# Weight sums at each stage's beginning, u one stage ahead, exponentials behind z's silu, and seven products for the first pool pair

## The chip, the cores and the metric

The kernel runs on one core of one Trainium2 chip. The metric is the device time in microseconds of one execution, the median of three runs. The engines of the core are named as in the profile: PE is TensorE (its matmuls; PEld are its weight loads), DVE is VectorE, ACT is ScalarE, POOL is GpSimd and SP is SyncE. Each engine works through its own queue in order; a DMA is issued from the queue of one of the engines, here SP, POOL or ACT.

## The reference, cut to what matters

512 tokens and 16 meta tokens ahead of them go through one layer of a hybrid decoder: a projection of all features, a pooling branch, a state-space branch (Mamba-2, "SSD") in 8 groups, gates that merge the two, and an MLP.

```
u = rmsnorm(h, mix_norm_w)
proj = u @ w_in                       # pool | z | x,B,C | dt | gates
u_pool, z, xbc, dt_raw, gates = ...
y_pool = pool_mixer(u_pool, pool_w_group, pool_scale) @ w_pool_up
# mamba2_branch
xbc = silu(causal_depthwise_conv(xbc, conv_w, conv_b))
xs, b_mat, c_mat = ...
y = ssd_chunked(xs, dt, a, b_mat, c_mat) + xs * d_skip
y = y * silu(z)
y = y * rsqrt(mean over the group(y * y) + EPS) * norm_w
y_ssd = y @ w_ssd_out
h = h + (gate_pool * y_pool + gate_ssd * y_ssd) @ w_o
v = rmsnorm(h, mlp_norm_w)
h = h + square(relu(v @ w_ff1)) @ w_ff2
out = rmsnorm(h, final_norm_w)
```

The pooling branch has four groups of 256 features with windows of 2, 4, 8 and 16 positions; each takes the windowed mean of its own projection less the projection itself, and then a 256 x 256 matrix.

## The kernel before

*Products.* Every float32 operand is split into a rounded part and the remainder (hi and lo), and a product is three matmuls: hi with hi, hi with lo and lo with hi. A weight block of 1024 columns is loaded by SP into a tile `raw` (three buffers), cast to `whi` by ACT (L95), and subtracted to `wlo` by DVE (L97); both have four buffers. Features lie on the 128 partitions, tokens (528, or 512 without the meta tokens) along the free dimension, in two halves of 264 columns where all 528 are wanted. L197 and L199 are the matmuls of `proj`.

*Seven products.* Two weight blocks against two halves of u can be multiplied with seven products of 264 columns instead of eight. It needs sums of the weight blocks (T1, T2, S3, T4) and sums of u (`T["0", ...]`, `T["1", ...]`). The function `pair` does this for the x tiles of groups 4 to 7 (`X_PAIRS`): all seven products write one psum tile `pqx` of two banks, and after each, ACT or DVE takes the bank's value into `rax` or `rbx`. The sums of the weights are formed in DRAM, by DMAs on POOL's queue that copy a block and then accumulate another onto it (`weight_steps`; tiles `f_t`, `f_s`, `fx_t`, `fx_s`); the sums for the two MLP matrices, used at the end of the kernel, are made in the same way. The sums of u are formed by `sums_of_u`: two raw tiles of u come in by DMA on POOL's queue (`rau`, `rbu` from `u_d`), DVE combines them in four operations (L876 to L879), and ACT and DVE split the results. The function `pool_pair` does seven products for two tiles of a pool group, with the weights' sums formed by DVE; before, the first pool group treated, group 3, has its two tiles by `pool_tile` instead, each with its own weight block against both halves of u, 48 matmuls of 264 columns.

*Stages.* Stage g runs the state-space part of group g, `ssd(g)`, together with `group_proj(g + 1)`, which projects B, C (`px`), the two x tiles (`px`, or `pqx` as a pair), a gate tile in some groups (`pgp`), and z (`pz`, two halves in one psum tile, then ACT's silu into `zt`). The function `weave` takes one step of each generator in turn; engines then run in the order of the program, unless `issue_after` puts an instruction behind a named one of its engine. `ssd(g)` begins with transposes (`ptb`, `ptm`, `ptx`), loads a broadcast of the cumulated decay (`abc`, 1 MB, on POOL's queue), takes exponentials of it (`eb`, L609; masks in `abc`, L614, L620, L621), computes the states (`pst`, copied to `st` at L643), the two parts of y (`po`, `py`), multiplies by z's silu into `yt`, squares it (`sqg`, split to `qhg`, L311, and `qlg`), sums the squares on PE (`png`, L685 and L686), takes the reciprocal root (`rs`, L688), and splits the normed y into `yh` (L697) and `yl`. ACT's functions are exp, silu and the reciprocal root, and a change between them is an ACT_TABLE_LOAD.

*Around the stages.* In stage 4 `out_half` is woven in: the product with the first half of `w_ssd_out`, eight tiles of 512 columns in `pso`, copied to `so` (L806) and put into DRAM. In stage 7 `out_part` (`psp`) fills the place of the projection. Then come the pool stage (four groups in the order 3, 2, 1, 0), the rest of the gates, the merge, `w_o`, and the MLP.

*Where the weight sums' DMAs stand.* `weight_sums_at(SETS_AT[g], PIECES.get(g, 12))` spreads the DMAs of one or two sets over a stage's steps. Each is ordered behind a copy of one column of the latest result (`seen`, on POOL), so that it is not issued before the stage has come that far. `SETS_AT` gives the sets of the eight stages: 1, 1, 2, 1, 2, 2, 1, 1. psum has two buffers for tiles of two banks (`psum2`) and four for tiles of one (`psum1`).

*Where the exponentials stand.* `eb` of group g comes behind the silu of that group's x tiles (`x_ready`), and for groups 5 to 7 behind that of z (`z_ready`):

```
with tc.issue_after((z_ready if g in X_PAIRS[1:] else x_ready)[g].ins):
    act.activation(eb[js, :, :], ap[js, :, j, :], AF.Exp)
```

Of the kernel before, what the change touches and what calls it, by code (L numbers as in the profile page):

```python
# [14 lines left out]
P = 128  # L15
# [31 lines left out]

SUMS_AT = {0: (0,), 1: (1,), 2: (2, 3)}

# [3 lines left out]

SETS_AT = {0: 1, 1: 1, 2: 2, 3: 1, 4: 2, 5: 2, 6: 1, 7: 1}
PIECES = {4: 21, 7: 14}
SETS_POOL = 0

# [7 lines left out]
def kernel(ctx: ExitStack, tc, xT, x, w, fx, f1, f2, vec, fnw, out):  # L65
# [110 lines left out]
    def psum2(name):  # L176
        return psa.tile([P, 1024], F32, tag="mm", name=name)
# [32 lines left out]
    def narrow(ps):  # L210
        return [(ps, slice(NM, L))]
# [200 lines left out]
    mark = [None]  # L412
    x_ready, z_ready, filled = {}, {}, {}

    def conv(dst, src, ct):
        n = dst.shape[-1]
        e = src.shape[-1] - n
        act.activation(dst, src[:, e:], AF.Identity, bias=col(V_CB, ct), scale=col(V_CW, ct * 4 + 3))
        for j in range(1, 4):
            o = max(0, j - e)  # L420
            dve.scalar_tensor_tensor(dst[:, o:], src[:, e + o - j : e + n - j],
                                     col(V_CW, ct * 4 + 3 - j), dst[:, o:], op0=ALU.mult, op1=ALU.add)
        silu = act.activation(dst, dst, AF.Silu)
        mark[0] = dst[:, :1]
        if ct < 16:
            x_ready[ct // 2] = silu

# [44 lines left out]
    def pair(kind, g, r):  # L472
# [5 lines left out]
        for m, f, n, start, stop in MULTIPLY:  # L478
# [3 lines left out]
            for low in range(2):  # L482
                for k in range(4):
                    wk = wt[low][:, k * P : (k + 1) * P]
                    pe.matmul(o, wk, f[k][0], start=start and not low and k == 0,  # L485
                              stop=stop and low == 1 and k == 3, skip_group_check=True)
                    if not low:
                        pe.matmul(o, wk, f[k][1], start=False, stop=False, skip_group_check=True)
# [19 lines left out]
    def group_proj(g, cur, gate=None):  # L508
# [60 lines left out]
    def ssd(g, cur):  # L569
# [36 lines left out]
        for j in range(2):  # L606
            js = slice(64 * j, 64 * j + 64)
            with tc.issue_after((z_ready if g in X_PAIRS[1:] else x_ready)[g].ins):
                act.activation(eb[js, :, :], ap[js, :, j, :], AF.Exp)  # L609
# [94 lines left out]
    def weave(a, b, n, sums, side):  # L704

        end = object()
        a, sums = [a], [sums]
        while a or b or side:
            for t in [a] + [b] * n:
                for q in (t, sums):  # L710
                    if q and next(q[0], end) is end:
                        q.pop(0)
            side = [q for q in side if next(q, end) is not end]
        for q in sums:
            for _ in q:
                pass
# [25 lines left out]
    def weight_steps():  # L742
        t = sets.pop(0)
        src = {"fx": fx, "f1": f1, "f2": f2}[t[0]][t[1]]
        o = {n: wsum[(*t, n)] for n in SUMS[t[0]]}
        put = nc.gpsimd.dma_start
        yield put(o["t1"], src[B11])
        yield put(o["s3"], src[B12])
        yield put(o["t1"], src[B12], accum_op=ALU.add)
        if "t2" in o:  # L750
            yield put(o["t2"], src[B22])
        yield put(o["s3"], src[B22], accum_op=ALU.add)
        if "t2" in o:
            yield put(o["t2"], o["t1"], accum_op=ALU.add)
            yield put(o["t4"], src[B21])
            yield put(o["t4"], o["t2"], accum_op=ALU.add)

# [4 lines left out]

    def weight_sums_at(n, pieces):
        total = sum(2 * len(SUMS[t[0]]) for t in sets[:n])
        steps = (e for _ in range(n) for e in weight_steps())
        put = i = 0
        while put < total:
            i += 1
            if put * pieces < i * total:
# [3 lines left out]
                put += 1  # L773
            yield
        assert next(steps, None) is None

# [23 lines left out]
    def out_half():  # L800
        for dd in range(4):
            ps = psum2(f"pso{dd}")
            for i in range(2):
                ssd_out(2 * dd + i, ps[:, i * SEQ : (i + 1) * SEQ], range(8))
                o = staged(f"so{2 * dd + i}")
                act.copy(o, ps[:, i * SEQ : (i + 1) * SEQ])  # L806
                nc.scalar.dma_start(acc_d[2 * dd + i], o)
                mark[0] = o[:, :1]
                yield
# [51 lines left out]


    def sums_of_u(ks, g):

        one, two = HF

        def load(k):
            a, b = raw_pair("u", k)
            with tc.issue_after(abc_load[g].ins):
                for t, kk in ((a, k), (b, k + 4)):  # L870
                    nc.gpsimd.dma_start(t, u_d[kk])
            return a, b

        def combine(a, b, behind):
            with tc.issue_after(behind[g].ins):
# [4 lines left out]

        def form(k, n, src, behind):
            hi, lo = T[n, "h", k], T[n, "l", k]
# [40 lines left out]
    yps, last, copied, mixed = {}, {}, {}, []  # L923

    def pool_tile(t):
        win = WIN[t // 2]
        ps = psum2(f"pp{t}")

        skip = min(NM - win, NM - 4)
        runs, view = wide(ps, skip)  # L930
        proj(runs, block(), U)
        u = gp.tile([P, L + 8], F32, tag="pu", name=f"pu{t}", bufs=4)[:, :L]
        act.copy(u[:, skip:], view)
        return averaged(t, u)

# [92 lines left out]
    for d in range(NK):  # L1028
        t_load = nc.gpsimd.dma_start(acc[d], acc_d[d])
    for _ in range(SETS_POOL):  # L1030
        with tc.issue_after(t_load.ins):
            t_load = weight_sums()
    pend = [pooled_halves(*pool_tile(2 * POOL_ORDER[0] + i)) for i in range(2)]

# [783 lines left out]
```

## Time and profile before

| | us |
|---|---|
| median of three runs | 1017.71 |
| lowest and highest | 1017.05, 1018.7 |
| profiled execution | 1019.7 |
| its span | 1018.0 |
| PE busy | 998.0 |
| PE weight loads busy | 876.6 |
| DVE busy | 799.0 |
| ACT busy | 603.6 |
| POOL busy | 120.4 |

The span is the time from the first to the last instruction of the profiled execution. Busy times of different engines overlap. Matmuls are pipelined, so one is drawn longer than the distance to the next one's start. A row of the time line gives the start, the duration, the engine, the line of the kernel, the operation and its tiles, how many like it follow one another (x), and in brackets how long the engine stood idle before it and what ended that. A row of the table of stretches gives each engine's busy time and its number of instructions, the clock that TensorE was granted (1.00 is full speed), the busy share of the 16 DMA engines, and GB/s.

### The profile page before, as it was taken

What the parts mean: (1) busy time and instruction counts of PE and PEld (TensorE: products, weight loads), DVE (VectorE), ACT (ScalarE), POOL (GpSimd) and SP (SyncE); (2) the same over time, 40 slices, a digit from 0 to 9 for tenths busy, and PEclk for the clock granted to TensorE, in tenths of its full rate; (3) what the DMA queues carried; (4) which work ended last, traced back from release to release, by engine and by line L of the source; (5) the groups of instructions that cost most, each with busy time, mean ns of one, the idle gap of its engine ahead of it and who ended that gap; (6) DMA issues with size and microseconds to landing.
All of it is one profiled execution on the core that took longest, in us unless ns stands there. A gap on an engine that the chain in (4) does not pass through costs nothing.

```text
span 1018.0 us, 15702 instructions
## 1 busy us (share of the span) xinstructions
PE 998.0 (98%) x6047; PEld 876.6 (86%) x6047; DVE 799.0 (78%) x1153; ACT 603.6 (59%) x853; POOL 120.4 (12%) x215
## 2 busy tenths in 40 slices
PE   9999999999999999999999999999999999999997
PEld 7889888979788897987889888888889999999986
DVE  7968797778653787877689756877988888888885
ACT  8656769484833575665345533458656656665654
POOL 0001211212122212123400000221000000000000
PEclk9999999999999999999999999999999999999999
DMA  7265868566688748487933542879454554455432
GB/s 254 87 225 163 246 192 229 167 188 198 179 255 266 215 140 238 118 233 208 253 129 103 212 161 63 268 193 338 112 185 134 158 182 149 156 175 150 141 104 83
DMA packets 61803, 184.52 MB, mean 181 GB/s; under 512 B 7072, under 2 KB 8416, under 8 KB 60704
## 3 DMA queue, kind: packets, MB, share of 16 engines
q1 hardware_dynamic: 39456, 109.00, 32.3%
q0 software_dynamic: 18240, 67.51, 26.2%
q10 hardware_dynamic: 4032, 7.00, 1.9%
q8 instruction: 47, 0.77, 0.3%
q14 instruction: 28, 0.23, 0.1%
HBM read 173.13 MB, written 58.59 MB: 228 GB/s over the span
## 4 chain that ended last, share of the span: by engine, by line
PE 87%; ACT 6%; DMA 3%; DVE 2%; issue 1%; POOL 0%; ACTq 0%; DVEq 0%; POOLq 0%; SPq 0%
PE px L1437 8%; PE px L197 7%; PE alpha L1505 6%; PE px L1440 4%; PE px L199 4%; PE pz L197 4%; PE alpha L1508 3%; PE pgs L197 3%; PE pgp L197 2%; DMA raw<-in_w 2%; PE pqx L485 2%; PE py L667 2%; PE pz L199 2%; PE wo_alpha L1199 1%; PE pf L130 1%; PE pf L129 1%
## 5 line engine op out<-in xcount | busy, mean ns | idle before, releaser
L95 ACT CAST whi<-raw 128x1024 fp32r<-128x1024 f32 (+2 forms) x90 | 90.1, 1011 | 83.4 <-DMA raw<-in_w 18.1
L97 DVE TENSOR_TENSOR wlo<-raw,whi 128x1024 fp32r<-128x1024 f32 (+2 forms) x90 | 104.9, 1172 | 37.9 <-ACT whi L95 28.9
L197 PE MATMUL px<-uh,whi 128*128 128x264 f32 (+1 forms) x320 | 82.4, 295 | 0.0
L199 PE MATMUL px<-ul,whi 128*128 128x264 f32 (+1 forms) x320 | 79.9, 287 | 0.0
L1212 DVE TENSOR_TENSOR ht<-ht,alpha 128x1024 f32<-128x1024 f32 x35 | 42.7, 1219 | 29.1 <-PE alpha L1505 29.1
L197 PEld LDWEIGHTS px<-uh,whi 128*128 128x128 f32 x320 | 61.5, 192 | 1.3 <-issue 0.9
L199 PEld LDWEIGHTS px<-ul,whi 128*128 128x128 f32 x320 | 61.3, 192 | 0.3
L1135 ACT CAST shi<-rawf 128x1024 fp32r<-128x1024 f32 x42 | 44.2, 1053 | 28.7 <-PE alpha L1508 18.3
L1505 PE MATMUL alpha<-shi,hh 128*128 128x512 f32 x140 | 55.2, 394 | 0.0
L1508 PE MATMUL alpha<-shi,hl 128*128 128x512 f32 x140 | 54.7, 391 | 0.0
L1136 DVE TENSOR_TENSOR slo<-rawf,shi 128x1024 fp32r<-128x1024 f32 x42 | 51.2, 1218 | 0.6 <-ACT shi L1135 0.6
L1440 PE MATMUL px<-vsl,shi 128*128 128x256 f32 x192 | 47.4, 280 | 0.0
L1437 PE MATMUL px<-vsh,shi 128*128 128x256 f32 x192 | 47.4, 281 | 0.0
L197 PE MATMUL pz<-uh,whi 128*128 128x512 f32 x112 | 45.1, 402 | 1.5 <-ACT yh L697 1.3
L199 PE MATMUL pz<-ul,whi 128*128 128x512 f32 x112 | 44.6, 398 | 0.0
L197 PE MATMUL px<-uh,wlo 128*128 128x264 f32 (+1 forms) x320 | 42.5, 284 | 0.0
L197 PEld LDWEIGHTS px<-uh,wlo 128*128 128x128 f32 x320 | 40.1, 189 | 0.0
L1505 PE MATMUL alpha<-slo,hh 128*128 128x512 f32 x140 | 37.4, 389 | 0.0
L1437 PEld LDWEIGHTS px<-vsh,shi 128*128 128x128 f32 x192 | 36.2, 188 | 0.9
L1440 PEld LDWEIGHTS px<-vsl,shi 128*128 128x128 f32 x192 | 36.1, 188 | 0.9
L1440 PE MATMUL px<-vl,shi 128*128 128x256 f32 x144 | 36.1, 283 | 0.0
L1437 PE MATMUL px<-vh,shi 128*128 128x256 f32 x144 | 36.0, 282 | 0.0
(600 smaller groups left out, 3066.5 us busy)
## 6 DMA issues: line engine op xcount, KB each, us to landing
raw<-in_w SPq DMA_DIRECT2D x96, 512.0 KB, 4.9
f_t<-in_f POOLq DMA_DIRECT2D x38, 512.0 KB, 6.8
f_s<-in_f POOLq DMA_DIRECT2D x26, 512.0 KB, 7.4
b<-in_f SPq DMA_DIRECT2D x21, 512.0 KB, 4.6
rawf<-in_f SPq DMA_DIRECT2D x36, 256.0 KB, 3.0
rawf<-f_t SPq DMA_DIRECT2D x36, 256.0 KB, 2.9
abc<-acs_d POOLq DMA_DIRECT2D x8, 1024.0 KB, 7.6
f_t<-f_t POOLq DMA_DIRECT2D x12, 512.0 KB, 5.9
```

Source lines behind the costliest of these rows:

```text
L95: act.copy(hi[:, c], raw[:, c])
L97: dve.tensor_tensor(lo[:, c], raw[:, c], hi[:, c].bitcast(F32), op=ALU.subtract)
L197: pe.matmul(o, wt, rhs[0][k][:, c], start=part == 0 and k == 0, stop=part == 1 and k == NK - 1)
L199: mm[0] = pe.matmul(o, wt, rhs[1][k][:, c], start=False, stop=False)
L485: pe.matmul(o, wk, f[k][0], start=start and not low and k == 0, stop=stop and low == 1 and k == 3, skip_group_check=True)
L1135: splits.append((act.copy(hi, src), dve.tensor_tensor(lo, src, hi.bitcast(F32), op=ALU.subtract)))
L1136: dve.tensor_tensor(lo, src, hi.bitcast(F32), op=ALU.subtract)))
L1212: added[0] = dve.tensor_tensor(o, o, src, op=op)
L1437: pe.matmul(ps, m, f[k][0], start=start and not low and k == 0, stop=stop and low == 1 and k == 3, skip_group_check=True)
L1440: pe.matmul(ps, m, f[k][1], start=False, stop=False, skip_group_check=True)
L1505: pe.matmul(ps[t], hh[:, p, seg, st], m, start=bool(first and not low and p == 0), stop=bool(last and low and p == 1), skip_group_check=True)
L1508: pe.matmul(ps[t], hl[:, p, seg, st], m, start=False, stop=False, skip_group_check=True)
```

## The change

- *Weight sums.* One generator, `line`, runs over all sets. `paced(slots)` issues a given number of its DMAs at given steps of a stage: five at step 0, two at step 2, one at step 4; stage 4 has eight more at steps 9, 12 and 14, and stage 7 only two and two. Each slot has one `seen` copy on POOL. Within a set, or within two sets of the second MLP matrix, all copies are issued ahead of the accumulations. The number of sets that go through is the same.
- *Sums of u.* `sums_of_u` runs in stages 0, 1 and 2 as before, but with two of the four in stage 0, and the load of the next raw tiles is issued at the end of a sum, so that it is there when the next stage wants it. In `weave` it takes its step after the step of `ssd` and ahead of the weight sums.
- *Exponentials.* `eb` comes behind z's silu in all groups.
- *z of groups 5 to 7.* The matmuls of z are ordered behind the last matmul of the pair (`paired_up`).
- *out_half.* Each of the eight tiles has its own psum tile.
- *First pool pair.* Pool group 3 goes through `pool_pair`, as the other three.

```diff
-SUMS_AT = {0: (0,), 1: (1,), 2: (2, 3)}
+SUMS_AT = {0: (0, 1), 1: (2,), 2: (3,)}
...
-SETS_AT = {0: 1, 1: 1, 2: 2, 3: 1, 4: 2, 5: 2, 6: 1, 7: 1}
-PIECES = {4: 21, 7: 14}
+SLOTS = {0: 5, 2: 2, 4: 1}
+SLOTS_LONG = {**SLOTS, 9: 4, 12: 2, 14: 2}
+SLOTS_LAST = {0: 2, 2: 2}
...
-                    pe.matmul(o, wk, f[k][0], start=start and not low and k == 0,
+                    paired_up[g] = pe.matmul(o, wk, f[k][0], start=start and not low and k == 0,
...
-            proj(narrow(ps), wt, X if first else U)
+            with tc.issue_after(paired_up[g].ins) if g in paired_up else nullcontext():
+                proj(narrow(ps), wt, X if first else U)
...
-            with tc.issue_after((z_ready if g in X_PAIRS[1:] else x_ready)[g].ins):
+            with tc.issue_after(z_ready[g].ins):
                 act.activation(eb[js, :, :], ap[js, :, j, :], AF.Exp)
...
+    def paced(slots):
+        for i in range(max(slots) + 1):
+            if i in slots:
                 at = pool.tensor_copy(seen, mark[0])
-                with tc.issue_after(at.ins):
-                    next(steps)
+                for _ in range(slots[i]):
+                    with tc.issue_after(at.ins):
+                        next(line)
             yield
...
     def out_half():
         for dd in range(4):
-            ps = psum2(f"pso{dd}")
             for i in range(2):
-                ssd_out(2 * dd + i, ps[:, i * SEQ : (i + 1) * SEQ], range(8))
+                ps = psum2(f"pso{2 * dd + i}")[:, :SEQ]
+                ssd_out(2 * dd + i, ps, range(8))
...
+    u_raw = []
     def sums_of_u(ks, g):
...
-        t = load(ks[0])
+        if g == 0:
+            load(0)
         yield
-        combine(*t, masked)
+        combine(masked)
         yield
-        form(ks[0], "0", t[0], y_first)
-        if len(ks) > 1:
-            form(ks[0], "1", t[1], y_first)
-            t = load(ks[1])
+        form(ks[0], 0, y_first)
         yield
+        form(ks[0], 1, y_first)
+        if ks[0] < 3:
+            load(ks[0] + 1)
         yield
         if len(ks) > 1:
-            combine(*t, squared)
-            form(ks[1], "0", t[0], squared)
+            combine(squared)
             yield
-        form(ks[-1], "1", t[1], squared)
+            form(ks[1], 0, squared)
+            yield
+            form(ks[1], 1, squared)
+            load(ks[1] + 1)
         yield
...
-        weave(ssd(g, cur), fill, 2 if g == 4 else 1, weight_sums_at(SETS_AT[g], PIECES.get(g, 12)),
+        weave(ssd(g, cur), fill, 2 if g == 4 else 1, paced({4: SLOTS_LONG, 7: SLOTS_LAST}.get(g, SLOTS)),
               [sums_of_u(SUMS_AT[g], g)] if g in SUMS_AT else [])
...
-    pend = [pooled_halves(*pool_tile(2 * POOL_ORDER[0] + i)) for i in range(2)]
+    pend = [pooled_halves(*a) for a in pool_pair(POOL_ORDER[0])]
```

More of the change, by code (lines that the diff above doesn't have):

```diff
@@ L708, in weave @@
         while a or b or side:
[L709 to L713, printed above, removed]
+            for i, t in enumerate([a] + [b] * n):
+                if t and next(t[0], end) is end:
+                    t.pop(0)
+                if i == 0:
+                    side = [q for q in side if next(q, end) is not end]
+                if sums and next(sums[0], end) is end:
+                    sums.pop(0)
         for q in sums:
@@ L867, in load, with combine @@
         def load(k):
-            a, b = raw_pair("u", k)
+            raw = raw_pair("u", k)
             with tc.issue_after(abc_load[g].ins):
-                for t, kk in ((a, k), (b, k + 4)):
+                for t, kk in zip(raw, (k, k + 4)):
                     nc.gpsimd.dma_start(t, u_d[kk])
-            return a, b
-        def combine(a, b, behind):
+            u_raw.append(raw)
+        def combine(behind):
+            a, b = u_raw[-1]
             with tc.issue_after(behind[g].ins):
@@ L879, in combine, with form @@
                 dve.tensor_tensor(b[:, one], b[:, one], a[:, one], op=ALU.add)
-        def form(k, n, src, behind):
-            hi, lo = T[n, "h", k], T[n, "l", k]
+        def form(k, i, behind):
+            hi, lo = T["01"[i], "h", k], T["01"[i], "l", k]
+            src = u_raw[-1][i]
             with tc.issue_after(behind[g].ins):
@@ L923 @@
     yps, last, copied, mixed = {}, {}, {}, []
[L925 to L934, printed above, removed]
     def averaged(t, u):
@@ L1029 @@
         t_load = nc.gpsimd.dma_start(acc[d], acc_d[d])
-    for _ in range(SETS_POOL):
-        with tc.issue_after(t_load.ins):
-            t_load = weight_sums()
-    pend = [pooled_halves(*pool_tile(2 * POOL_ORDER[0] + i)) for i in range(2)]
+    assert next(line, None) is None
+    pend = [pooled_halves(*a) for a in pool_pair(POOL_ORDER[0])]
     un = units()
```

50 lines of the change are left out of this document (21 added, 29 removed).

## The prediction, made before the changed kernel had run

> **What bounds the kernel now.** I read the shares and the chain first, then TensorE's waits, then the time line around each wait, and the table by stretches last.
>
> ```profile
> PE 998.0 (98%) x6047; PEld 876.6 (86%) x6047; DVE 799.0 (78%) x1153; ACT 603.6 (59%) x853; POOL 120.4 (12%) x215
> PE 87%; ACT 6%; DMA 3%; DVE 2%; issue 1%; POOL 0%; ACTq 0%; DVEq 0%; POOLq 0%; SPq 0%
> ```
>
> TensorE (PE) is busy for 98% of the span and makes 87% of the chain that ended last. So there are two ways to win: fewer matmuls, or fewer of the few places where PE stands still. PE's waits, as line, what it waited for, total, times, longest:
>
> ```profile
> PE pso L129 <- ACT so L806: 2.5, 1, 2.5
> PE png L685 <- ACT qhg L311: 2.2, 2, 1.8
> PE ptx L597 <- DVE xddm L590: 1.8, 2, 1.5
> PE psp L850 <- ACT whi L818: 1.2, 1, 1.2
> PE png L686 <- DVE qlg L312: 0.7, 2, 0.5
> PE pst L641 <- DVE xdd L602: 0.3, 1, 0.3
> ```
>
> They lie at the ends of the group stages. PE's time line at four of them (start, duration, operation; in brackets the idle time before and what ended it):
>
> ```profile
> 131.36 0.38 PE L661 MATMUL po<-ct,st 128*128 128x128 f32 x2
> 133.24 0.99 PE L667 MATMUL py<-abc,xdt 128*64 128x128 f32 x14 [1.50 <-issue]
> ...
> 205.97 0.50 PE L685 MATMUL png<-qhg,ones_r 128*128 128x512 f32 x1 [1.77 <-ACT qhg L311]
> 206.69 0.50 PE L686 MATMUL png<-qlg,ones_r 128*128 128x512 f32 x1 [0.22 <-DVE qlg L312]
> 207.46 0.76 PE L197 MATMUL pz<-uh,whi 128*128 128x512 f32 x1 [0.26 <-DVE xc L421]
> ...
> 280.31 0.50 PE L129 MATMUL pso<-yh,whi 128*128 128x512 f32 x1 [2.55 <-ACT so L806]
> ...
> 404.83 0.44 PE L597 MATMUL ptx<-ident,xc 128*128 128x128 f32 x2 [1.53 <-DVE xddm L590]
> ```
>
> In the next view each row is a stretch: PE, weight loads, VectorE (DVE), ScalarE (ACT) and GpSimd (POOL) busy, then PE's granted clock, the busy share of the DMA engines, and GB/s.
>
> ```profile
> 86.00:94.00 8.00, 7.64 (x65) 6.85 (x64) 7.48 (x14) 6.24 (x9) 0.81 (x2) 1.00 0.18 68
> 206.00:214.00 8.00, 7.51 (x24) 5.66 (x25) 6.43 (x9) 7.44 (x9) 3.36 (x6) 0.79 0.74 245
> 274.00:282.00 8.00, 5.45 (x29) 4.44 (x28) 3.35 (x4) 7.82 (x15) 3.07 (x4) 1.00 0.63 164
> 390.00:398.00 8.00, 8.00 (x44) 6.79 (x44) 6.27 (x8) 3.94 (x5) 0.00 (x0) 1.00 1.03 382
> 406.00:414.00 8.00, 8.00 (x56) 7.95 (x56) 7.67 (x15) 7.92 (x16) 1.25 (x3) 0.82 0.83 229
> ```
>
> Two of the stalls are followed by a lowered clock: 8 us x (1 - 0.79) = 1.7 us are lost after the one at 206, 8 x (1 - 0.82) = 1.4 us after the one at 404, near 1.7 with the fraction before 406. The stall at 277 to 280 leaves the clock at 1.00. The DMA engines are full at 390 to 398 and nearly empty at 86 to 94, the early part of a stage. What was late at the stalls, on DVE and on ACT:
>
> ```profile
> 201.42 0.43 DVE L876 TENSOR_TENSOR rbu<-rau,rbu 128x264 f32<-128x264 f32 x1 [4.03 <-DMA rbu<-u_d]
> ```
> ```profile
> 122.37 1.28 ACT L609 ACT_TABLE_LOAD   x1
> 123.66 1.05 ACT L609 ACTIVATE eb<-abc 64x1024 f32<-64x1024 f32 x1
> 130.72 0.35 ACT L643 COPY st<-pst 128x256 f32<-128x256 f32 x1
> ...
> 279.70 0.56 ACT L806 COPY so<-pso 128x512 f32<-128x512 f32 x1
> ...
> 398.52 1.05 ACT L95 CAST whip<-rawp 128x1024 fp32r<-128x1024 f32 x1 [3.81 <-DMA rawp<-in_fx]
> ```
>
> **The change, part by part.** *Transfers and u.* At 201.42 DVE had stood 4.03 us in front of the combine of u, whose raw tile came by GpSimd's queue among weight sums; the square of y, qhg and the norm's matmuls (205.97) stood behind it. At 398.52 ACT had stood 3.81 us before the cast of the pair's weights, whose load was issued into the full stretch 390 to 398; z's silu and the transposes (404.83) were late by it. After the change the same transfers go out in stage slots 0, 2 and 4 (five, two, one), in the thin part, and u is loaded a stage earlier. I therefore let both stalls go: 1.77 + 0.22 + 0.26 = 2.25 and 1.8 us (both waits of ptx). Each bracket is too small by about 0.16 us, since a matmul is drawn longer than its pitch (0.39 drawn, 0.23 from start to start, in the pz rows below): with five brackets 0.8 more. With the clock's 1.7 + 1.7 that is 8.2 us. Bounds: nothing, if the loads are late again, to 8.2; I take all, since DVE and ACT would have been ready 4 us earlier and PE needed 2.3. The GpSimd work loses 40 or so tiny copies, off the path.
>
> The price of it is in the early part: eight 512 KB transfers in a row share the DMA engines with the weight loads.
>
> ```profile
> raw<-in_w SPq DMA_DIRECT2D x96, 512.0 KB, 4.9
> f_t<-in_f POOLq DMA_DIRECT2D x38, 512.0 KB, 6.8
> ```
>
> A weight block lands 4.9 us after issue, a sum's copy 6.8. Three raw buffers stand ahead of PE, and a block of 32 + 16 matmuls of 264 columns takes 48 x 0.12 = 5.8 us, so a load may land 5 to 10 us late before PE runs dry. I take nothing here; the bound above is that every stage loses one landing's difference (6.8 - 4.9 = 1.9), 7 x 1.9 = 13 us.
>
> *Exponentials behind z's silu.* In the early groups ACT runs exp, silu, rsqrt, exp, each change of function with a table load; the second half of eb, of 1.05 us, starts at 123.66, and the copy of the state (130.72) comes at the end of that row of work. PE waited for it at 131.36 to 133.24. With both halves behind the silu, the first exp and its load and the return to silu (two loads) leave the row ahead of the copy: the copy comes about 128.0 instead of 130.7, and PE asks for it at 131. The load of the row at 122.37 took 1.28, so two are 2.6 us and the stall of 1.5 goes (+0.16). The same shortening ends the other waits of the table: png 2.2 - 1.8 = 0.4 and 0.7 - 0.22 = 0.5, psp 1.2, pst 0.3, and 0.16 for each, 2.9 us together. Bound: nothing to these 4.5. The Trainium skill ("ScalarE: Activation LUTs", section "What ACT_TABLE_LOAD costs") adds a drain of about 1.38 us to the load's 1.283. This trace disagrees: the eb half at 123.66 starts at the end of the load (122.37 + 1.28). By the page two loads would be worth 5.3 us on ACT, and PE would still gain only its 1.5.
>
> *A psum tile for each half of out_half.* The second product of a tile waited for the copy of the first (279.70), because both halves were one tile. Apart, they alternate between two buffers: 2.55 + 0.35 (the row's end is a short matmul, drawn long) = 2.9 us gone. Bounds 2 to 2.9.
>
> *First pool pair by seven products.* It had 96 matmuls of 264 columns, now 7 x 12 = 84:
>
> ```profile
> 493.09 0.28 PE L197 MATMUL pp<-uh,whi 128*128 128x264 f32 x1
> 493.21 0.29 PE L199 MATMUL pp<-ul,whi 128*128 128x264 f32 x1
> ```
> ```profile
> L965 DVE TENSOR_TENSOR sm<-raw,raw 128x512 f32<-128x512 f32 x3 | 2.1, 686 | 1.0 <-DMA raw<-in_w 1.0
> ```
>
> 12 x 0.12 = 1.4 us less on PE. DVE gets four sums of 0.69, 2.7 us, hidden behind the out_part matmuls ahead of the pair, as the weights are prefetched; without that cover PE would wait for the sums' split, 2.7. Bounds -1.4 to +1.3; I take -1.4.
>
> *z's matmuls held behind the pair's last product (groups 5 to 7).* This one costs. The seven products of an x pair all write one psum tile, so each waits for the eviction of the one before, even in the other bank. Before, z's matmuls ran in these gaps (stage of group 5, PE, then ACT):
>
> ```profile
> 341.93 0.65 PE L485 MATMUL pqx<-t0h,wlop 128*128 128x264 f32 x4
> 342.42 0.39 PE L197 MATMUL pz<-uh,whi 128*128 128x512 f32 x1
> 342.65 0.40 PE L199 MATMUL pz<-ul,whi 128*128 128x512 f32 x1
> ...
> 343.12 0.34 PE L485 MATMUL pqx<-t1h,whip 128*128 128x264 f32 x1
> ...
> 344.13 0.66 PE L485 MATMUL pqx<-t1h,wlop 128*128 128x264 f32 x4
> ...
> 345.79 0.31 PE L485 MATMUL pqx<-t0h,whip 128*128 128x264 f32 x1
> ```
> ```profile
> 342.62 0.39 ACT L494 ACTIVATE rbx<-pqx 128x264 f32<-128x264 f32 x1 [1.68 <-PE pqx L485]
> ...
> 344.33 1.05 ACT L95 CAST whi<-raw 128x1024 fp32r<-128x1024 f32 x1 [1.33 <-PE pqx L488]
> 345.29 0.37 ACT L496 COPY rbx<-pqx 128x264 f32<-128x264 f32 x1
> ```
>
> The product ends at 342.58, its eviction runs from 342.62 to 343.01, and the next starts at 343.12. Its last matmul started at 341.93 + 3 x 0.12 = 342.29; at a pitch of 0.12 the next could have started at 342.41, so an empty gap costs 0.7 us. Where ACT has a cast first (344.33, of 1.05) it is 345.79 - 344.61 = 1.2. The changed order leaves five gaps of group 5 without a filler: one small (0.2), three of 0.7, one of 1.2, 3.5 us. Group 6 has three (2.2), group 7 has four, two of them behind a cast (2.9). The z matmuls run afterwards at their usual pitch, so nothing comes back: +8.6 us. Bounds: 15 gaps at an eviction's 0.39 with little latency, 4.5, to all of them behind a cast, 12 x 1.2 = 14.
>
> *Small new waits.* In group 2 the norm's matmuls now stand ahead of z's, and the exponentials come later for yt: two or three waits of the size of the 0.2 to 0.5 in the tables, +1.0 (0 to 2).
>
> *The sum*: -8.2 - 4.5 - 2.9 - 1.4 + 8.6 + 1.0 = -7.4 us. The profiled execution took 1019.7 (span 1018.0, 1.7 around it), 2 above the median 1017.71, so it becomes 1012.3, and the median 1010.3.
>
> **Rivals.** *A, as above:* 1010.3; with the bounds of the smaller terms 1007 to 1014.
>
> *B, slower: the clock falls in the pairs.* Products of 12 x 0.12 = 1.4 us with 0.7 to 1.2 empty leave PE idle for a third of a stretch of 13 us in each of three pairs. A lowered stretch costs 1.7 (above). The place is the x pair of groups 5 to 7, four stretches of the length of a drop (2 x 1.7 = 3.4 us) in each; five drops of the twelve already undo the 7.4, and six give 1010.3 + 10.2 = 1020.5. For it: PE has no filler there. Against it: at 274 to 282, 32% idle (5.45 of 8.00 busy), the clock stayed at 1.00, and the two drops came behind an idle of two thirds of such a stretch (2.25 of 3.4). The Trainium skill ("TensorE: Matmul & The Clock Gate", section "A second HAM failure mode: psum-queue depth-cycling") speaks for B: matmul groups that cycle through PSUM leave small idles often enough for the clock gate to oscillate. The trace has such a cycle only with fillers, so it neither confirms nor denies it.
>
> *C, the gaps cost less:* evictions run on a less loaded engine because z's silu is later, and an empty gap costs about 0.4, 4.5 in all: 1006.2.
>
> *D, the transfers only move:* the burst at a stage's start delays u's or the pair's loads as before, and both stalls stay. 1010.3 + 8.2 = 1018.5. For it: landings of 6.8 against 4.9, and the early part also has weight loads. Against it: 0.18 busy at 86 to 94.
>
> **How the numbers follow.** A 0.48, C 0.14, D 0.22, B 0.13, and 0.03 for a late split of the pool pair on top of D (about 1021). A difference under 0.2% (2 us) can't be told from none: faster means under 1015.7, slower over 1019.7. All of A and C are faster, and half of D, where one of two stalls goes (1014.4); of the rest of D most is the same, a third slower. Faster 0.73, same 0.08, slower 0.19. The likeliest time is 1010.3, its own range 1007 to 1014; the range for 8 in 10 takes C's value and D's: 1004 to 1019.5.
>
> **What would show it.** Right: no wait over 0.5 us at the ends of groups 1, 3 and 5, clock 1.00 throughout stages 3 and 5; no wait of pso for so; 84 matmuls of the first pool pair; new waits of PE's pqx for the evictions, some 8 us in all and the largest entry of its waits. Wrong: pqx waits near 4 (C) or a clock under 0.95 in the pairs' stretches (B); DVE waiting for u_d or ACT for rawp by 2 us or more (D); ACT waiting for raw in the first third of the stages by more than now; a PE wait on whiS or wloS in the first pool pair.

## The result, and the profile after

| | before | after |
|---|---|---|
| median of six runs, us | 1017.38 | 1024.66 |
| lowest and highest | 1014.89, 1019.77 | 1022.47, 1026.22 |
| span of the profiled execution | 1018.0 | 1024.5 |

The ratio is 1.0059, with a 95% interval of 1.0033 to 1.0084: the change makes the kernel slower by 0.6%, where 0.7% faster was forecast. First the engines' busy time on the page of the changed kernel, then its waits of PE (line, what it waited for, total, times, longest):

```profile
PE 998.8 (97%) x6035; PEld 878.9 (86%) x6035; DVE 805.3 (79%) x1162; ACT 599.5 (59%) x853; POOL 102.2 (10%) x173
```
```profile
PE pz L197 <- ACT rax L501: 3.4, 1, 3.4
PE pz L197 <- DVE wlo L97: 3.3, 1, 3.3
PE pqx L483 <- ACT rbx L494: 2.8, 3, 0.9
PE pz L197 <- ACT gp L730: 2.6, 1, 2.6
PE pqx L483 <- DVE rbx L497: 1.6, 3, 0.6
PE pqx L483 <- DVE rax L490: 1.5, 1, 1.5
...
PE pqx L483 <- DVE rbx L499: 0.5, 1, 0.5
PE pqx L483 <- ACT rbx L492: 0.5, 1, 0.5
```

The waits shown before (pso, most of png, ptx, psp) are gone from this list. Two kinds have come: pqx, as predicted, 2.8 + 1.6 + 1.5 + 0.5 + 0.5 = 6.9 us, and three single waits of pz, 9.3 us, which were not. Where the three lie, in PE's time line and then in the table of stretches (the columns are those shown before):

```profile
116.26 2.00 PE L197 MATMUL pz<-uh,wlo 128*128 128x512 f32 x5 [3.35 <-DVE wlo L97]
...
161.84 0.77 PE L197 MATMUL pz<-uh,whi 128*128 128x512 f32 x1 [2.64 <-ACT gp L730]
...
263.60 0.77 PE L197 MATMUL pz<-uh,whi 128*128 128x512 f32 x1 [3.44 <-ACT rax L501]
```
```profile
116.00:124.00 8.00, 7.54 (x39) 6.38 (x40) 7.32 (x12) 5.39 (x7) 1.58 (x4) 0.79 0.77 217
156.00:164.00 8.00, 5.36 (x23) 4.27 (x22) 3.64 (x5) 5.36 (x7) 0.00 (x0) 0.83 0.79 282
204.00:212.00 8.00, 7.91 (x42) 6.42 (x40) 6.25 (x9) 4.66 (x6) 0.00 (x0) 1.00 0.94 339
260.00:268.00 8.00, 4.55 (x13) 3.57 (x13) 6.14 (x8) 5.83 (x8) 0.00 (x0) 0.79 0.54 163
340.00:356.00 16.00, 11.93 (x87) 10.63 (x87) 10.68 (x16) 8.80 (x14) 2.07 (x3) 1.00 0.65 166
```

They stand at the ends of stages 0, 1 and 3, and each has a lowered clock behind it in this trace (0.79, 0.83, 0.79). The end of stage 2 (204 to 212) is now at full clock and nearly full, as predicted. In the pair of group 5 (340 to 356) PE is idle for 4 of 16 us, and the clock is 1.00 all the same.

To set the two kernels against each other, one matmul's start is subtracted from the next one's, and the median pitch for its number of columns (0.227 us for 512, 0.121 for 264, and so on) from that; what is left over is lost time, summed by place. The lowered clock is in it.

| place | before, us | after, us |
|---|---|---|
| end of stage 0 (110 to 140) | 3.1 | 6.1 |
| end of stage 1 (150 to 170) | 0.8 | 4.3 |
| end of stage 2 (200 to 220) | 4.6 | 0.7 |
| end of stage 3 and the first pso (250 to 280) | 3.9 | 5.5 |
| pair of group 5 (330 to 360) | 2.4 | 5.8 |
| pair of group 6 and the stage's end (380 to 410) | 4.1 | 2.1 |
| pair of group 7 (420 to 450) | 0.0 | 3.4 |
| first part of stage 7 (450 to 470) | 3.9 | 1.3 |
| all of it, with the rest | 30.1 | 38.1 |

8.0 us more are lost and the matmuls take 12 x 0.121 = 1.45 less: 6.55 in sum, and the spans differ by 1024.5 - 1018.0 = 6.5. ("By starts" below means a loss taken in this way, from one start to the next.)

### The profile page after: what moved, and what is told of

The parts are those of the page before. It is cut to its first block, busy times and chain, and to the rows that moved or that the text cites. A ratio compares the mean times of both kernels' runs of the same rounds, so it can differ in the third digit from the quotient of the medians.

```text
span 1024.5 us, 15612 instructions
## 1 busy us (share of the span) xinstructions
PE 998.8 (97%) x6035; PEld 878.9 (86%) x6035; DVE 805.3 (79%) x1162; ACT 599.5 (59%) x853; POOL 102.2 (10%) x173
## 4 chain that ended last, share of the span: by engine, by line
PE 88%; DMA 4%; DVE 3%; ACT 3%; issue 1%; POOL 0%; ACTq 0%; DVEq 0%; SPq 0%; POOLq 0%
PE px L1432 8%; PE alpha L1500 6%; PE px L197 6%; PE pz L197 5%; PE px L1435 4%; PE alpha L1503 3%; PE px L199 3%; PE pgs L197 3%; PE pz L199 3%; PE pqx L483 2%; DMA raw<-in_w 2%; PE pgp L197 2%; PE py L666 1%; PE pf L130 1%; PE pso L129 1%; PE pf L129 1%
## 5 line engine op out<-in xcount | busy, mean ns | idle before, releaser
L97 DVE TENSOR_TENSOR wlo<-raw,whi 128x1024 fp32r<-128x1024 f32 (+2 forms) x88 | 102.4, 1171 | 44.3 <-ACT whi L95 28.1
L95 ACT CAST whi<-raw 128x1024 fp32r<-128x1024 f32 (+2 forms) x88 | 87.9, 1010 | 79.0 <-DMA raw<-in_w 25.4
```

What stands on the lines that cost most here:

```text
L95: act.copy(hi[:, c], raw[:, c])
L97: dve.tensor_tensor(lo[:, c], raw[:, c], hi[:, c].bitcast(F32), op=ALU.subtract)
```

## The experiments

Each median was taken beside runs of the kernel before on the same chip, and the kernel before itself came to medians of 1017.4 to 1019.7 there; so the ratio to the kernel before is what is compared. A difference of medians in us can carry up to 2 us of that.

| run | what it is | median, us | ratio, interval |
|---|---|---|---|
| the change | all parts | 1024.66 | 1.0059 (1.0033 to 1.0084) |
| e1 | the change, z not held | 1023.22 | 1.0052 (1.0029 to 1.0075) |
| e2 | the change, u as before | 1016.68 | 0.9969 (0.9947 to 0.9991) |
| e3 | the change, sums as before | 1020.61 | 1.0026 (1.0004 to 1.0049) |
| e4 | the change, exponentials as before | 1018.28 | 0.9993 (0.9972 to 1.0014) |
| e5 | before + exponentials | 1019.41 | 1.0006 (0.9986 to 1.0026) |
| e6 | before + u ahead | 1014.40 | 0.9963 (0.9944 to 0.9983) |
| e7 | before + slots | 1012.01 | 0.9935 (0.9914 to 0.9955) |
| e8 | e2, two psum tiles in a pair | 1016.07 | 0.9970 (0.9944 to 0.9996) |
| e9 | before + slots + u ahead | 1017.17 | 0.9985 (0.9959 to 1.0011) |
| e10 | the change, last slot of stage 0 behind u | 1021.34 | 1.0025 (1.0005 to 1.0045) |
| e11 | e7 + halves of out_half + pool pair | 1012.05 | 0.9926 (0.9905 to 0.9947) |
| e12 | e11 + exponentials | 1022.07 | 1.0025 (1.0005 to 1.0046) |
| e13 | e11 + z held | 1017.49 | 0.9983 (0.9959 to 1.0007) |
| e14 | e12, one slot | 1016.31 | 0.9963 (0.9925 to 1.0001) |
| e15 | the change, one slot | 1017.90 | 0.9998 (0.9972 to 1.0023) |
| e16 | e11, one slot | 1016.80 | 0.9970 (0.9950 to 0.9991) |
| e17 | e15, z not held | 1009.88 | 0.9910 (0.9881 to 0.9939) |
| e18 | e17, exponentials as before | 1014.57 | 0.9968 (0.9947 to 0.9988) |

### One part of the change undone

e1:

```diff
-            with tc.issue_after(paired_up[g].ins) if g in paired_up else nullcontext():
-                proj(narrow(ps), wt, X if first else U)
+            proj(narrow(ps), wt, X if first else U)
```

> The changed kernel with z's matmuls of groups 4 to 7 no longer held behind the pair's last product. Theory H (the hold costs the empty gaps): in the changed kernel the starts of pqx matmuls after a gap add up to 4.8 + 1.8 + 2.1 = 8.7 us in the stages of groups 5, 6 and 7; they go, and the time falls by 7 to 9 from 1024.7 to about 1016.5. Rival (z, run afterwards, saves as much elsewhere): within 3 of 1024.7.

The gaps went, but the time fell by only 1.4, which the intervals can't tell from nothing. In its trace, 1.4 us near 340 and some 3 near 455, which the hold had taken away by moving z, are back, and a wait of 1.9 in the first pool pair with a lowered stretch behind it has come. The three stalls of pz stay (2.0, 3.3 and 3.2 us by starts), but only the last has a lowered clock behind it. (The change also holds z of group 4, in stage 3; the stall at 260 stays without that.) So the hold is not what makes the change slower than the kernel before.

e2, with `sums_of_u` and its loads as before:

```diff
-SUMS_AT = {0: (0, 1), 1: (2,), 2: (3,)}
+SUMS_AT = {0: (0,), 1: (1,), 2: (2, 3)}
...
-            u_raw.append(raw)
+            return a, b
```

> The changed kernel with the sums of u as before (one pair of tiles in stages 0 and 1, two in stage 2, each loaded in its own stage). Theory U (the stall of 3.5 us at 112.5 and the lowered clock behind it come from the second pair of u, which stage 0 now loads just ahead of its use): DVE's wait for u_d at 111.6 (5.95 us) and that stall are gone, a wait for u_d in stage 2 near 200 comes back with 2 us or more; in sum 1020 to 1026. Rival S (the sums' slots are at fault): the stall near 112 stays over 2 us.

Theory U: the stall at 112 is gone, and so is the one at 260. The wait for u_d in stage 2 came back on DVE, as expected, but PE does not stall behind it:

```profile
200.78 0.43 DVE L877 TENSOR_TENSOR rbu<-rau,rbu 128x264 f32<-128x264 f32 x1 [2.77 <-DMA rbu<-u_d]
```

One stall, of 1.7 and 0.5 with a lowered stretch, is left at the end of stage 1. The time fell by more than expected, under the kernel before.

e3, with the functions and sets of before, and the order of `weave` of before:

```diff
-paced({4: SLOTS_LONG, 7: SLOTS_LAST}.get(g, SLOTS))
+weight_sums_at(SETS_AT[g], PIECES.get(g, 12))
```

> The changed kernel with the weight sums' transfers spread over the stages as before. Theory S (three transfers of sums stand at the end of the stage, together with abc and the u loads, so ACT gets its raw blocks late): the stalls at 158.9 (2.8) and 259.8 (3.6), each with 1.7 of lowered clock, go, the time falls by 5 to 9 to about 1018; a wait of ACT for rawp near 400 comes back (up to 3.7). Rival (the exponentials or u are at fault for these two): the stalls stay, 1024 or more.

Theory S in part: the time fell by less than it said. The stalls at 112 and 159 are gone, and ACT waits 2.3 us for rawp again. At the end of stage 3, 2.7 us come for a product of the pair and 2.0 for pz, at stage 2's end 1.7, and 2.2 in the first pool pair.

e4:

```diff
-            with tc.issue_after(z_ready[g].ins):
+            with tc.issue_after((z_ready if g in X_PAIRS[1:] else x_ready)[g].ins):
```

> The changed kernel with the exponentials of groups 1 to 4 behind the silu of x as before. If the exponentials' place gave what the prediction said, the wait for the copy of the state near 131 to 137 comes back with about 1.5, the time 1026. If ACT is late at 158.9 and 259.8 because of it, these stalls shrink, and the time falls to 1020.

The second: the stall at 260 is gone, the one at 159 is down to 1.8 us in three pieces, the one at 112 (3.6) stays. No stall came back at 131. By the medians, undoing any one of three parts (u, the slots, the exponentials) takes half of the loss or more away, so it is no part's price; they make it together. For the slots (e3) the interval still overlaps that of the change.

### One part alone

e5, e6 and e7 put one part each into the kernel before:

```diff
 # e5
-            with tc.issue_after((z_ready if g in X_PAIRS[1:] else x_ready)[g].ins):
+            with tc.issue_after(z_ready[g].ins):
 # e6, with the change's sums_of_u
-SUMS_AT = {0: (0,), 1: (1,), 2: (2, 3)}
+SUMS_AT = {0: (0, 1), 1: (2,), 2: (3,)}
 # e7, with the change's weight_steps, line and paced
-weight_sums_at(SETS_AT[g], PIECES.get(g, 12))
+paced({4: SLOTS_LONG, 7: SLOTS_LAST}.get(g, SLOTS))
```

> The kernel before with only the exponentials of groups 1 to 4 behind z's silu. Theory E (the exponentials' place is good by itself, it only costs beside late raw blocks): the wait for st at 131 (1.5) goes, the time is 0 to 3 under before. Rival (ACT's later exponentials delay psum evictions at the ends of stages 1 and 3 by themselves): new waits of pz at 157 and 257 of over 2 us, 3 to 6 over before.

Neither expectation by itself: the stall at 131 goes, one of 2.5 at 256 comes, with a lowered clock, and the time is the same.

> The kernel before with only the sums of u a stage ahead, two pairs in stage 0. Theory U: DVE waits near 105 to 112 for u_d by 3 us or more, PE stalls by 2 to 4 near 112 with a lowered clock behind it; the stall at 203.8 with its lowered clock (1.9 + 1.0 + 1.7) goes; in sum -2 to +3. Rival (the load is only late where the sums' slots stand ahead of it in GpSimd's queue): no wait for u_d near 112, 3 to 5 under before.

The rival: no stall near 112, full clock in all stages, 0.37% faster. Without the slots' accumulations in the queue the second u load goes out at 101.8 and 102.8 and is there when DVE asks for it at 106.8. The stall at 131 is gone here too, with the exponentials where they were.

> The kernel before with only the weight sums' transfers in slots. If the slots by themselves free the loads, the stalls at 203.8 (1.9) and 402.9 (1.8) go with their lowered clocks: 5 to 8 under before. Rival (the accumulations of the later slots and the 1 MB of abc meet at the end of the stage): ACT's waits for raw grow from 18 to 25 us, PE stalls by 2 or more at 158 or 258: within 3 of before.

The first theory: 0.65% faster, and both lowered stretches are gone. New is a wait of 2.1 for st near 90: in stage 0 u's first load now stands behind slot 0's four copies and one accumulation. The wait of pso for so went too, without the change to out_half.

### Two parts together, and their order

e9 is e7 with e6's edit as well.

> The kernel before with two parts, the sums' slots and u a stage ahead, which alone gave 0.9935 and 0.9963 of its time. Theory Q (the two are bad together: in stage 0 the second u load stands in GpSimd's queue behind an accumulation that waits for its source): DVE waits 4 to 6 us for u_d near 110, PE stalls by 3 or more near 112 with a lowered clock, and the time is 1015 to 1019. Rival (they add up): 0.990, some 1008 to 1010.

Theory Q: each part alone is faster, and together they are even with the kernel before. DVE waits 9.4 us for u_d, 7.2 at once, and the clock is low for 10 us behind it. (e9 keeps the order of `weave` of the kernel before, so u's first load stands behind slot 0 as in e7, and the wait for st near 92, 2.0, is there too.) The queue of GpSimd in the changed kernel shows why:

```profile
93.54 0.18 POOL L772 COPY seen<-st 128x1 f32<-128x1 f32 x1 [11.17 <-DVE st L648]
94.04 0.85 POOL L760 DMA_DIRECT2D fx_s<-in_fx  x1 [0.31 <-issue]
94.57 1.14 POOL L760 DMA_DIRECT2D fx_t<-fx_t  x1
98.39 0.57 POOL L576 DMA_DIRECT2D abc<-acs_d  x1 [2.67 <-issue]
99.59 0.18 POOL L772 COPY seen<-yt 128x1 f32<-128x1 f32 x1 [0.63 <-DVE yt L673]
103.42 0.82 POOL L760 DMA_DIRECT2D fx_t<-fx_t  x1 [3.64 <-DMA fx_t<-fx_t]
103.96 0.86 POOL L874 DMA_DIRECT2D rau<-u_d  x1
104.52 0.85 POOL L874 DMA_DIRECT2D rbu<-u_d  x1
```

and the changed kernel's DVE:

```profile
111.64 0.43 DVE L880 TENSOR_TENSOR rbu<-rau,rbu 128x264 f32<-128x264 f32 x1 [5.95 <-DMA rbu<-u_d]
```

Slot 2 (behind st, 93.5) and slot 4 (behind yt, 99.6) are late in the stage, not at its beginning. The accumulation of slot 4 waits 3.64 us at the head of the queue until the one whose sum it adds has landed; u's second load stands behind it, lands 7 us after its issue, beside abc, and holds DVE for 5.95.

e10 lets the load pass:

```diff
-paced({4: SLOTS_LONG, 7: SLOTS_LAST}.get(g, SLOTS))
+paced({0: {0: 5, 2: 2, 6: 1}, 4: SLOTS_LONG, 7: SLOTS_LAST}.get(g, SLOTS))
```

> The changed kernel with the last accumulation of stage 0 behind the second u load in GpSimd's queue (slot 6 in place of 4, in stage 0 alone). Theory Q: DVE's wait of 5.95 falls by the 3.6 that the queue stood, the stall at 112.5 (3.5) under 1 and no lowered clock there, the time 1018 to 1021. Rival (the DMA engines are full with abc and the copies, the order changes nothing): the wait stays over 4, 1023 or more.

Theory Q again: DVE's wait is 0.9, the stall at 112 and its lowered clock are gone, and the time is 3.3 less, with intervals that overlap. The other two stalls stay: they have another cause.

### The slots and the exponentials

e11 is e7 with the halves and the pool pair as in the change, e12 is e11 with e5's edit:

```diff
-            ps = psum2(f"pso{dd}")
...
+                ps = psum2(f"pso{2 * dd + i}")[:, :SEQ]
...
-    pend = [pooled_halves(*pool_tile(2 * POOL_ORDER[0] + i)) for i in range(2)]
+    pend = [pooled_halves(*a) for a in pool_pair(POOL_ORDER[0])]
```

> The kernel before with the sums' slots, a psum tile for each half of out_half, and the first pool pair by seven products. If the pool pair gives its 12 matmuls (1.4) and the slots give what they gave alone: 1010 to 1011.5 against 1012. Rival (raw blocks behind the loads of acc come late in the pool pair, as at 497 in two runs before): a wait of pz for whi or wlo of 1.5 or more near 490, 1012 to 1014.

Even with e7: the pool pair's 1.4 us and out_half's tiles bring nothing that can be told from the noise, since the wait of pso was gone in e7 and 0.9 is waited for in the first pool pair.

> The kernel of the run before with the exponentials of groups 1 to 4 behind z's silu as well. Alone they changed nothing (1.0006): the stall at 131 went, one at 256 came, as the copy of the pair's last product then stands behind a cast that waits for its raw block. If that mechanism holds here too, waits of pz for rax or gp of 2 us or more at 157 or 257 come, and the time is 2 to 6 over the run before. Rival (with the slots, raw blocks land in time at these ends): the stall of 1.7 near 135 goes, 1 to 2 under it.

What costs nothing alone costs 10 us beside the slots, more than expected. By e12's trace not all of it is the mechanism expected. PE waits 3.1 us at 160 for qhg, which stands on ACT behind a cast of a late block; 2.7 at 213 for xc, which DVE makes after a wait for u_d; 1.2 at 263 for rax; and 3.5 in the first pool pair, where the edit moves nothing, again behind a late block on ACT, with a lowered clock (0.79 at 504 to 512). ACT, then DVE, then ACT of e12:

```profile
158.66 1.04 ACT L95 CAST whi<-raw 128x1024 fp32r<-128x1024 f32 x1 [4.67 <-DMA raw<-in_w]
159.62 0.61 ACT L311 CAST qhg<-sqg 128x512 fp32r<-128x512 f32 x1
```
```profile
211.83 0.43 DVE L876 TENSOR_TENSOR rbu<-rau,rbu 128x264 f32<-128x264 f32 x1 [3.94 <-DMA rbu<-u_d]
```
```profile
503.75 1.04 ACT L95 CAST whi<-raw 128x1024 fp32r<-128x1024 f32 x1 [4.56 <-DMA raw<-in_w]
504.70 0.37 ACT L996 COPY pu<-pz 128x264 f32<-128x264 f32 x1
```

How much of the 10 us is the exponentials' own is not settled. The changed kernel's ACT at the end of stage 3 shows how a late block reaches PE:

```profile
256.87 1.05 ACT L95 CAST whi<-raw 128x1024 fp32r<-128x1024 f32 x1 [1.73 <-DMA raw<-in_w]
258.37 1.05 ACT L95 CAST whi<-raw 128x1024 fp32r<-128x1024 f32 x1 [0.46 <-DMA raw<-in_w]
259.32 0.82 ACT L418 ACTIVATE xc<-rbx,vs 128x528 f32<-128x528 f32 x1
262.22 1.05 ACT L95 CAST whi<-raw 128x1024 fp32r<-128x1024 f32 x1 [2.07 <-DMA raw<-in_w]
263.17 0.37 ACT L501 COPY rax<-pqx 128x264 f32<-128x264 f32 x1
```

The copy of the pair's last product takes 0.37 us and could have run at 260.1; it stands behind a cast that waits for its raw block, and PE waits for the psum tile. At 159 the same happens with the gate (gp). In the kernel before, with the exponentials earlier, the same copy (255.71) stood ahead of the cast that waited longest (258.42), and PE did not stall:

```profile
254.76 1.05 ACT L95 CAST whi<-raw 128x1024 fp32r<-128x1024 f32 x1 [0.82 <-DMA raw<-in_w]
255.71 0.38 ACT L503 COPY rax<-pqx 128x264 f32<-128x264 f32 x1
258.42 1.05 ACT L95 CAST whi<-raw 128x1024 fp32r<-128x1024 f32 x1 [2.33 <-DMA raw<-in_w]
```

Whether the landings or ACT's order decide was the next question; e15, e14 and e16 have this edit in the change, in e12 and in e11:

```diff
-SLOTS = {0: 5, 2: 2, 4: 1}
+SLOTS = {0: 8}
...
-SLOTS_LAST = {0: 2, 2: 2}
+SLOTS_LAST = {0: 4}
```

> The changed kernel with all eight transfers of a stage in slot 0. Theory C and Q: the second u load of stage 0 has no accumulation ahead of it, DVE's wait for u_d falls from 5.95 under 2, the stalls at 112, 159 and 260 (9.9 us and three lowered stretches, 5) go for the larger part; the gaps of 8.7 stay: 1012 to 1016 from 1024.7. Rival (the exponentials' order on ACT is enough): 1020 or more.

The landings, with ACT's order as in the change. ACT of e15 at the same place, with the same instructions in the same order:

```profile
247.18 1.05 ACT L95 CAST whi<-raw 128x1024 fp32r<-128x1024 f32 x1 [0.74 <-DMA raw<-in_w]
248.47 1.05 ACT L95 CAST whi<-raw 128x1024 fp32r<-128x1024 f32 x1 [0.24 <-DMA raw<-in_w]
249.43 0.82 ACT L418 ACTIVATE xc<-rbx,vs 128x528 f32<-128x528 f32 x1
250.16 1.03 ACT L95 CAST whi<-raw 128x1024 fp32r<-128x1024 f32 x1
251.09 0.36 ACT L501 COPY rax<-pqx 128x264 f32<-128x264 f32 x1
```

The raw blocks of these three casts landed 5.9, 6.0 and 8.6 us (least, median, most) after their issue in the changed kernel (issued at 250 to 254) and 4.7, 4.8 and 5.1 in e15 (241.5 to 245.5):

```profile
DMA to landing us min/median/max: 5.9/6.0/8.6
```
```profile
DMA to landing us min/median/max: 4.7/4.8/5.1
```

In the kernel before three blocks at this place (issued at 241 to 250) took 7.2, 7.9 and 9.2 us, without a stall. So it takes both: a late block, and a copy that stands behind its cast.

PE's waits in e15:

```profile
PE psp L129 <- ACT sp L839: 3.5, 1, 3.5
PE pqx L483 <- ACT rbx L494: 2.8, 3, 0.9
PE pqx L483 <- DVE rbx L497: 1.6, 3, 0.6
```

All three stalls of pz are gone or under 1 us, DVE waits 1.7 for u_d, the gaps of the pairs stay, and the time is that of the kernel before, 2 over the range expected; a wait of 3.5 for a psum tile of out_part is new.

> The kernel e12 (slots, halves, pool pair, exponentials behind z) with all eight transfers of a stage in slot 0. Theory C (the accumulations of slots 2 and 4 run into abc and the raw blocks at the stage's end, raw lands after 7 to 9 us and ACT's casts stand ahead of what PE waits for): ACT's waits for raw fall from 25 to under 17, the stalls at 157 (3.3), 210 (2.9), 263 (1.4) shrink to under 2 in all, the time from 1022 to 1011 to 1014. Rival (ACT's order alone makes them): 1019 or more, the stalls stay.

The stalls at 157, 210 and 263 come to 1.2, and the time falls by 6, less than expected: in stage 0 six of the eight transfers stand ahead of u's first tile and a seventh ahead of its second (this accumulation holds the queue for 6.64 us before the second tile is issued), DVE waits 6.1 for u_d, and PE stalls by 5.1 near 94, with two lowered stretches. The queue of GpSimd in e14:

```profile
90.79 0.83 POOL L759 DMA_DIRECT2D fx_t<-fx_t  x1 [6.64 <-DMA fx_t<-in_fx]
91.33 0.87 POOL L871 DMA_DIRECT2D rbu<-u_d  x1
```

> The kernel e11 with all eight transfers of a stage in slot 0. If the later slots cost something there too (u_d is waited for 3.2 us, a stall of 2.2 at 90.6 and a lowered stretch), 1008 to 1011; otherwise within 2 of 1012.

Slower than e11, for the same stall near 94. The cause is the order of `weave`: e7, e9, e11 to e14 and e16 take the weight sums' step ahead of u's, so u's first load stands behind slot 0. The change takes u's step first and issues this load at 71.3, ahead of slot 0 (75.7); e2, which has that order and loads u in its own stage, does not stall there. So, as far as these runs show, one slot is only good with u's load ahead of it.

### The pairs' gaps

> The changed kernel with the sums of u as before, and each of the pair's two accumulators in a psum tile of its own. Theory H (the gaps between the products are waits for the eviction of the other bank of the same tile): the starts of pqx after a gap, 8.7 us in the stages of groups 5 to 7, fall under 2, the time from 1016.7 to about 1010. Rival (the eviction of the same bank is what it waits for, or the held second tile stops pz): within 3 of 1016.7.

```diff
-        ps = psum2(f"pq{kind}{g}")
-        banks = (ps[:, :HALF], ps[:, 512 : 512 + HALF])
+        banks = tuple(psum2(f"pq{kind}{g}_{i}")[:, :HALF] for i in range(2))
```

The gaps fell from 8.7 to about 2 (0.6, 0.3 and 1.1 in group 5, none in the others): the wait is for the other bank of the same tile. The time hardly moved (the rival's range): 1.4 came back near 428 and 451 each, and a wait of 1.6 in the first pool pair.

e13 is e11 with the change's `paired_up`:

> The kernel e11 with z's matmuls held behind the pair's last product as well. Theory H, in a kernel with few other stalls: 8.7 us of gaps come, the waits at 338 (1.4) and those near 450 (1.4 and 0.4) go as the ends move: net 4 to 7 over e11's 1012. Rival (the hold frees as much elsewhere, as taking it out of the changed kernel gave only 1.4): within 2 of e11.

5.4 us (0.57% by the ratios), as theory H had it. The pqx waits of e13 are those of the changed kernel:

```profile
PE pqx L485 <- ACT rbx L496: 2.8, 3, 0.9
```

### Both faults taken away

e17 is e15 with e1's edit, e18 is e17 with e4's.

> The changed kernel with all eight transfers of a stage in slot 0 and z not held. If the gaps (8.7) go as in e13 against e11 (5.4 net), 1011 to 1014 from e15's 1017.9, the fastest with all of u, exponentials and slots. Rival (what the hold gave up elsewhere comes back, as in e1): 1016 or more.

Faster than expected, 0.9% under the kernel before, and the lowest median of all. PE's waits in e17:

```profile
PE pz L980 <- ACT pu L992: 2.6, 1, 2.6
PE pdt L241 <- DVE ones_r L140: 1.5, 1, 1.5
PE pz L197 <- ACT rax L501: 1.3, 1, 1.3
PE pz L197 <- ACT yh L695: 1.3, 1, 1.3
```

> The kernel of the run before with the exponentials of groups 1 to 4 behind the silu of x as before. If their place costs only beside late raw blocks: within 2 of the run before. If it costs by itself: 2 to 5 under it, 1007 to 1011, under the 1012 of the best so far.

Neither: with the exponentials where they were in the kernel before, it is 4.7 slower. ACT waits 43.8 us for raw blocks instead of 21.8, and stalls at the ends of stages 1 and 2 are back. So their place behind z's silu gains, once the transfers are out of its way. Whether all of the 4.7 is ACT's order, or the transfers fall otherwise as well, was not taken apart. e11 and e17 overlap in their intervals; which of the two is the faster isn't settled.

## Why the prediction was wrong

*The step that failed* is the first, "after the change the same transfers go out in stage slots 0, 2 and 4 (five, two, one), in the thin part". Slots are steps of the program, each behind a copy of a result. Only slot 0 (75.7) is early, and it goes out ahead of the thin stretch (86 to 94, DMA share 0.18); slots 2 and 4 are 18 and 24 us later, behind it, beside abc and the weight blocks of the stage's end. The shares around it in the kernel before were 0.66 ahead and 0.81 behind:

```profile
78.00:86.00 8.00, 8.00 (x63) 7.79 (x62) 5.18 (x13) 7.92 (x14) 0.00 (x0) 1.00 0.66 245
102.00:110.00 8.00, 8.00 (x42) 6.83 (x41) 6.76 (x9) 2.04 (x3) 1.05 (x2) 1.00 0.81 283
```

The time line of the kernel before could have told: behind which result each `seen` copy stands, and when that result came, is there. With it fell "and u is loaded a stage earlier": for the second pair of stage 0 this is not so, and nothing was said of the accumulation ahead of it in the queue (3.64 us; e10 takes the stall at 112 away by letting the load pass). All eight transfers in slot 0 (e15) take all three stalls away.

*The price taken at nothing.* The bound of one landing's difference for each stage, 13 us, was there, but was looked for in the early part, and given to rival D as a failure of the two gains. The place was the stage's end. What it cost: by starts the three stalls are 3.5 + 2.8 + 3.6 = 9.9 us, and the three lowered stretches behind them 3 x 1.7 = 5.1. The forecast of -7.4 with these 15.0 is +7.6; the spans differ by +6.5.

*The gains that were right.* At stage 2's end 3.9 us went (2.25 of waits and 1.7 of lowered clock forecast); the wait for rawp at 398 went, with PE's 1.8 and its lowered clock of 1.7; the pso wait of 2.9 is gone, but e7 shows that the slots alone take it away (in e5 and e6, too, 0.3 is left of 2.5), so it wasn't the separate psum tiles' to give. The end of stage 0 lost its wait for st, under a larger one. The pool pair saved its 1.45 and gave 0.7 back in a wait for pu.

*The exponentials* were priced at -4.5 as a shorter row on ACT. Of the waits in that sum only the one at 131 is theirs (1.67 by starts, gone in e5), and u a stage ahead takes it away as well (e6). The wait of psp stays in e5 (1.2); it is the hold of z that takes it away (gone in e13, back in e1). The exponentials also changed ACT's order: casts of blocks that are still on their way now stand ahead of copies out of psum. Alone that is even (e5), beside late blocks the time is 10 us longer (e12 against e11, not all of it by this path), and with timely ones it is shorter (e17 against e18).

*The hold of z* was right in mechanism, and in size as a sum: the gaps are 4.8 + 1.8 + 2.1 = 8.7 us by starts, where 3.5 + 2.2 + 2.9 = 8.6 was forecast, so part of the agreement is luck. "Nothing comes back" was wrong: the net price is 5.4 (e13 against e11) and 8.0 (e17 against e15), but 1.4 in the changed kernel (e1), where other stalls come in its place.

*Rival B* is refuted at its place: in the pairs the clock was 1.00 with a quarter of the time idle. Lowered stretches came instead behind single stalls of 2.8 to 3.6 us at the ends of the stages. The Trainium skill ("TensorE: Matmul & The Clock Gate", section "Part 1: The HAM clock gate") states a free-running window of 3.4 us. That agrees with stalls of one size being followed by a lowered clock (159, 2.8 us by starts) or not (e1 near 160, 3.3; e15 near 459, 3.7).

## What to carry to other kernels

Before a transfer is called early, find the result that it is ordered behind and the time of that result in the trace, and read what stands behind it in its queue: an accumulation that waits for its source holds every later load. On an engine that works in order, a short copy that frees a psum tile is only as early as the last landing that a cast ahead of it waits for. Parts of a change that use the same queues don't add up: two that gain 0.65% and 0.37% alone gained nothing together here.

## What was not expected of the hardware

A quarter of a 16 us stretch idle in gaps of 0.6 to 1.7 us left the granted clock at 1.00, while one stall of 2.8 us was followed by a lowered one. Another of 3.3 (e1, near 160) was not. An accumulating DMA that depends on another DMA held the queue of its engine for 3.64 us, in e14 for 6.64. 512 KB weight blocks at the end of stage 3 landed 4.7 to 5.1 us after their issue in e15 and 5.9 to 8.6 in the changed kernel, where accumulations in DRAM ran beside them.
